# 512-column products in two steps of 256 columns

## Chip, cores and metric

The kernel runs on one core of one Trainium2 chip. The metric is the device time of one launch in microseconds (us), lower is better. Instruction times come from one profiled execution. A core has five engines that run side by side and wait for one another through semaphores: TensorE (PE, matrix products; its loads of the stationary operand are listed apart as PEld), VectorE (DVE), ScalarE (ACT), GpSimd (POOL) and SyncE (SP, which here issues the DMAs).

## The reference

One decoder layer on a sequence of 512 tokens of width 1024, in float32. Two groups of attention heads read the same normalised input through one projection; their outputs are concatenated and go through one output projection; a gated channel mixer of width 2816 follows.

```python
h = rms_norm(x, attn_pre_norm[l])
mix = hybrid_mixer(h, l, w_in[l], ..., w_out[l])   # proj = h @ w_in; two head groups; concat @ w_out
x = x + rms_norm(mix, attn_post_norm[l])
h = rms_norm(x, ffn_pre_norm[l])
f = (jax.nn.silu(h @ w_gate[l]) * (h @ w_up[l])) @ w_down[l]
x = x + rms_norm(f, ffn_post_norm[l])
```

## The kernel before

**Products in three terms.** Each float32 operand is split into a rounded part ("hi", type fp32r, made by ScalarE) and the rest ("lo", made by VectorE). A product of two operands is then three matmuls into the same accumulator: hi·hi, lo·hi and hi·lo. A matmul multiplies a stationary operand of 128 × 128 (loaded by a weight load of its own, so each matmul in the profile has one) with a moving operand of 128 partitions and up to 512 columns, and adds the result to a PSUM tile of 128 × 512, which is one bank. Eight such tiles exist (tag "b", `ps`).

**Order.** The kernel writes out its order by hand: `PLAN` and `PLAN_NORM` are lists of step names, and `run` calls one Python function for each, in that order, on all engines. Behind the colon of a step stand the slots that its tiles take, so every tile has a fixed address. Two steps that follow each other on one engine are executed in the order of the list; between engines, semaphores order reads and writes of tiles.

**Stages**, by the times of the profile:

- *Input projection* (6 to 126 us). The transposed input, 8 slices `xh[k]`/`xl[k]` of 128 × 512, is the moving operand; the weights are stationary. For the first six output tiles (`FIRST`) the weights come in blocks by slice k, and `product_piece` (L572) makes one matmul per step `F{m}.{c}.{k}`: tile m, term c, slice k. For the ten others, `product_fm` (L589) makes the 8 matmuls of one term per step `F{m}.{c}`. Among these run matmuls of the compressed keys (L804, 256 columns) and, in the other orientation with weights moving, the value projections (L705, 256 or 280 columns).
- *Attention* (to about 250 us): scores (L922, L923), transposes (L953), products with the values (L1136 and others). Four tiles of the output projection's first half are made here by `mix_part` (L1207, steps `M0` to `M3`): 12 matmuls of 512 columns each, from `MIX_A`, which `mix_keep` then copies out.
- *Output projection* (250 to 284 us): `mix_piece(i, k)` calls `mix_final` (L1221) for one row block i and one slice k; for each half c of the 1024 output columns it makes the three terms. Row blocks 0 and 1 take the four slices that `mix_part` left out, 2 and 3 all eight (`MIX_K`).
- *Gate and up projections* (284 to 500 us): `block` (L1474) in a scheme that needs seven instead of eight block products per pair. Its moving operands have 256 columns already.
- *Down projection* (from 493 us): `product` (L1548) makes two PSUM tiles (t = 0, 1) of three terms each from a pair of feature tiles, called by `product_a` four times and by `product_b` three times for each of nine pairs. The last four feature tiles go through `down` (L1697): one row block i, one half c, three terms. The pieces of the last quarter are made by `down_piece` (L1703), which has 256 columns already. Then sums, the norm and the output follow on VectorE and ScalarE (L1719 to L1755).

**Flags.** A matmul with `start=True` begins a bank anew: columns that are written first afterwards are set, not added to. So where two matmuls begin the two halves of a bank, only the first has the flag; L1474 does so already.

Of the kernel before, what the change touches and what calls it, by code (L numbers as in the profile page):

```python
# [17 lines left out]
P = 128  # L18
# [3 lines left out]
NK = D_MODEL // P  # L22
# [16 lines left out]
NF = D_FF // P  # L39
# [209 lines left out]
MIX_A = (0, 1, 4, 5)  # L249
# [4 lines left out]
NA = 2  # L254
WB = (3, 3, 3)
HALVES = ((0, 256), (256, 512))
LAST = 1
SLOT = 1.43
AHEAD = 3
# [25 lines left out]
def hybrid_block_kernel(  # L285
# [6 lines left out]
    act, dve, pool, pe = nc.scalar, nc.vector, nc.gpsimd, nc.tensor  # L292
# [101 lines left out]
    def sslot(name, dt=F32R):  # L394
        return S.tile([P, SEQ], dt, tag="s", name=name)
# [6 lines left out]
    def ps(name, dt=F32):  # L402
        return PS.tile([P, SEQ], dt, tag="b", name=name)
# [11 lines left out]
    raws, fms = {}, {}  # L415
    st = {}
# [125 lines left out]
    blk = {}  # L542
# [24 lines left out]
    def product_piece(m, c, k):  # L567
        first = ("fm", m) not in st
        if first:
            st["fm", m] = ps(f"fm{m}")  # L570
        w, xx = ((1, xh), (2, xh), (1, xl))[c]
        pe.matmul(st["fm", m], blk[k][w][:, m * P:(m + 1) * P], xx[k], start=first, stop=True, skip_group_check=True)  # L572

    def high_fm(m):
        hi = wpool.tile([P, 1024], F32R, tag="hi", name="whi", bufs=WB[1])
# [8 lines left out]
    def product_fm(m, c):  # L584
        if c == 0:
            st["fm", m] = ps(f"fm{m}")
        w, xx = ((0, xh), (1, xh), (0, xl))[c]
        for k in range(NK):
            pe.matmul(st["fm", m], fms[m][w][:, k * P:(k + 1) * P], xx[k], start=(c == 0 and k == 0),  # L589
                      stop=(c == 2 and k == NK - 1))  # L590

    wide_of = {}

# [52 lines left out]
    for pair in range(8):  # L646
        scale = SCALE if pair in (DQ0, DQ1, NQ0, NQ1) else 1.0
        for half in range(2):
            m = 2 * pair + half
# [330 lines left out]
    oth, otl = {}, {}  # L980
# [218 lines left out]
    wos = [None] * NK  # L1199
    mixp, mixq, mixw = [None] * (2 * NT), {}, [None] * 2  # L1200

    def mix_part(m, c):
        i, n = m // 2, 0
        pt = mixq[m] = ps("mixp")
        for k in MIX_A:
            for o, wi in ((oth, 0), (otl, 0), (oth, 1)):
                pe.matmul(pt, o[k][:, i * P:(i + 1) * P], wos[k][wi][c], start=(n == 0), stop=(n == 3 * len(MIX_A) - 1))  # L1207
                n += 1

    def mix_keep(m):  # L1210
        if mixw[m // 4] is None:
# [4 lines left out]
    def mix_final(i, mix, kts, first, last):  # L1216
        for c in range(2):
            n = 0
            for k in kts:
                for o, wi in ((oth, 0), (otl, 0), (oth, 1)):  # L1220
                    pe.matmul(mix[c], o[k][:, i * P:(i + 1) * P], wos[k][wi][c],  # L1221
                              start=(first and n == 0), stop=(last and n == 3 * len(kts) - 1))
                    n += 1

    kst, opair = [None] * GROUPS, {}
    for h in range(DIFF_HEADS):
        c = h // 2
# [61 lines left out]
    CS = [slice(c * SEQ, (c + 1) * SEQ) for c in range(2)]  # L1289
# [254 lines left out]

    def product(acc, a, b, first, last):
        for t in range(2):
            for n, (x, y) in enumerate(((0, 0), (1, 0), (0, 1))):
                pe.matmul(acc[t], a[x][:, t * P:(t + 1) * P], b[y],  # L1548
                          start=(first and n == 0), stop=(last and n == 2))

    accs, oa, ob, back4, ffx = {}, [{} for _ in range(NF)], [{} for _ in range(NPAIR)], {}, {}
    part, wc = {}, {}
# [137 lines left out]
    def quarter(i, c):  # L1690
        return accs[((1, 5), (7, 6))[i > 1][c]][i % 2]

    def down(f, i, c):
        o = HS * (i < 2) + (i % 2) * P
        first = f == 2 * NPAIR and c == 1 and i > 1
        for n, (a, wi) in enumerate(((0, 0), (1, 0), (0, 1))):
            pe.matmul(quarter(i, c), ffx[f][a][:, o:o + P], oa[f]["w"][wi][:, CS[c]],  # L1697
                      start=(first and n == 0), stop=(f == (NF - 3 if (i, c) == (LAST, 0) else NF - 1) and n == 2))

    def down_piece(f, h):  # L1700
        o = HS + LAST % 2 * P
        for n, (a, wi) in enumerate(((0, 0), (1, 0), (0, 1))):
# [11 lines left out]
    def piece(t, h):  # L1714
        return t if h is None else t[:, HALVES[h][0]:HALVES[h][1]]

# [6 lines left out]
    def out_tiles(i):  # L1723
        if i not in wc:
            wc[i] = [cpool.tile([P, 4], F32, tag="ssc", name="ss", bufs=NT), sslot("uf", F32), sslot("uf", F32)]
            if not junk and i in (0, LAST):
                junk.extend(sslot("uj", BF16) for _ in range(2))
        return wc[i]

    def last_square(i, c, h=None):  # L1730
        out_tiles(i)
        j = (1 - c) + (h or 0)
        sq = junk[c] if i in (0, LAST) else wc[i][1 + c].bitcast(BF16)
        act.activation(piece(sq[:, :SEQ], h), piece(part[i, c], h), AF.Square,
# [7 lines left out]
    def last_root(i):  # L1742
        r = cpool.tile([P, 1], F32, tag="rsc", name="rs", bufs=NT)
        j = 1 + (i == LAST)
        rsqrt_last(r, wc[i][0][:, j:j + 1], 1.0 / D_MODEL, wc[i][0][:, 3:4])
        wc[i].append(r)

    def last_gain(i, c):
        u = out_tiles(i)[1 + c]
        (nc.gpsimd if (i, c) == (LAST, 1) else dve).tensor_tensor(u, part[i, c], gains[2][:, CS[c]], OP.mult)  # L1750

# [64 lines left out]
    for f in range(NF + 1):  # L1816
        order = ((6, f), (5, f), (4, f - 1), (7, f), (3, f), (1, f + 1), (2, f + 1))
        for j, (n, ff) in enumerate(order):
            t = f * T + j * SLOT
            if (n, ff) == (4, NF - 1):  # L1820
                t = f * T - SLOT
# [3 lines left out]
    for f in range(NF):  # L1825
        b = f * T
# [23 lines left out]
    for p in range(NPAIR):  # L1850
        b = (2 * p + 2) * T
# [8 lines left out]
    for p in range(NPAIR):  # L1860
        b = te + 4 * p * D - 7.0
# [16 lines left out]
    for p in range(NPAIR):  # L1878
        b = tb + p * 3 * D - 6.0
# [19 lines left out]
    for f in range(2 * NPAIR, NF):  # L1899
# [3 lines left out]
        b = tc_ + (-15, -8, -3, 2)[g]  # L1903
# [3 lines left out]
    n = 0  # L1907
# [4 lines left out]
    for i in (2, 3, 0, 1):  # L1912
        for c in (1, 0):
# [8 lines left out]
            t = tc_ + n * D / 2  # L1922
# [3 lines left out]
            for h in pieces or (None,):  # L1926
                a = () if h is None else (h,)
# [100 lines left out]
```

## Time and profile before

| | us |
|---|---|
| median of three runs | 617.48 |
| lowest and highest | 616.74, 618.58 |
| profiled execution | 616.08 |
| its span, first to last instruction | 614.3 |

| engine | busy us | share of the span | instructions |
|---|---|---|---|
| PE | 604.1 | 98% | 4065 |
| PEld | 547.6 | 89% | 4065 |
| DVE | 545.9 | 89% | 965 |
| ACT | 373.4 | 61% | 784 |
| POOL | 101.5 | 17% | 153 |

The profile page shows these and the chain of work that ended last: at each step it goes back to what released an instruction, or to the instruction ahead of it on its engine. 86% of that chain is PE, 8% DVE, 3% DMA. Matmuls are pipelined: one starts before the one ahead of it has ended, so the sum of durations is more than the time they take, and the distance between starts is what counts. The mean granted clock of TensorE is 0.998.

### The profile page before, as it was taken

What the parts mean: (1) busy time and instruction counts of PE and PEld (TensorE: products, weight loads), DVE (VectorE), ACT (ScalarE), POOL (GpSimd) and SP (SyncE); (2) the same over time, 40 slices, a digit from 0 to 9 for tenths busy, and PEclk for the clock granted to TensorE, in tenths of its full rate; (3) what the DMA queues carried; (4) which work ended last, traced back from release to release, by engine and by line L of the source; (5) the groups of instructions that cost most, each with busy time, mean ns of one, the idle gap of its engine ahead of it and who ended that gap; (6) DMA issues with size and microseconds to landing.
All of it is one profiled execution on the core that took longest, in us unless ns stands there. A gap on an engine that the chain in (4) does not pass through costs nothing.

```text
span 614.3 us, 11002 instructions
## 1 busy us (share of the span) xinstructions
PE 604.1 (98%) x4065; PEld 547.6 (89%) x4065; DVE 545.9 (89%) x965; ACT 373.4 (61%) x784; POOL 101.5 (17%) x153
## 2 busy tenths in 40 slices
PE   8999999999999999999999999999999999999995
PEld 5888888899999989889999999999999978888884
DVE  5888988997899885899999999899999899989977
ACT  6436365476898986568585645555554566667522
POOL 0030000306868789200000000000000000000000
PEclk9999999999999999999999999999999999999999
DMA  8557788656342311644253443335342554576413
GB/s 260 194 196 276 272 271 283 230 189 208 105 120 87 103 36 35 206 171 147 94 159 117 138 138 123 119 125 184 122 138 86 172 172 161 185 247 230 137 41 132
DMA packets 38341, 98.41 MB, mean 160 GB/s; under 512 B 4240, under 2 KB 11792, under 8 KB 37392
## 3 DMA queue, kind: packets, MB, share of 16 engines
q1 hardware_dynamic: 38144, 97.59, 47.6%
q8 instruction: 32, 0.52, 0.3%
q14 instruction: 21, 0.17, 0.1%
q10 hardware_dynamic: 144, 0.13, 0.1%
HBM read 82.10 MB, written 15.60 MB: 159 GB/s over the span
## 4 chain that ended last, share of the span: by engine, by line
PE 86%; DVE 8%; DMA 3%; ACT 1%; issue 1%; SPq 0%; DVEq 0%
PE yz L1474 25%; PE acc L1548 13%; PE fm L589 9%; PE mix L1221 5%; PE x L1474 4%; PE fm L572 4%; PE tr L953 4%; PE avn L1136 3%; PE g L705 2%; PE sc L922 2%; PE sc L923 2%; PE mixp L1207 2%; PE v L705 2%; PE cmp L804 1%; PE av L1014 1%; PE acc L1697 1%
## 5 line engine op out<-in xcount | busy, mean ns | idle before, releaser
L1750 POOL TENSOR_TENSOR uf<-c,gain 128x512 f32<-128x512 f32 x1 | 1.3, 1283 | 353.4 <-DVE c L1719 353.4
L936 ACT ACTIVATE p<-sc,nm 128x256 f32<-128x256 f32 (+3 forms) x96 | 50.2, 530 | 13.8 <-DVE nm L932 13.5
L1474 PE MATMUL yz<-rope,wbh 128*128 128x256 f32 x352 | 47.1, 276 | 0.0
L932 DVE TENSOR_REDUCE nm<-sc 128x1 f32<-128x384 f32 (+3 forms) x96 | 42.9, 481 | 4.3 <-PE sc L928 3.7
L1105 POOL TENSOR_TENSOR p<-p,l 128x256 f32<-128x256 f32 (+3 forms) x64 | 45.3, 732 | 0.9
L1474 PEld LDWEIGHTS yz<-rope,wbh 128*128 128x128 f32 x352 | 43.2, 188 | 0.0
L966 DVE TENSOR_TENSOR ptl<-tr,pth 128x384 fp32r<-128x384 f32 (+1 forms) x60 | 34.2, 590 | 8.9 <-ACT pth L963 8.7
L963 ACT ACTIVATE pth<-tr 128x384 fp32r<-128x384 f32 (+1 forms) x60 | 30.3, 528 | 6.8 <-PE tr L953 6.5
L1451 ACT ACTIVATE wbh<-wraw 128x1024 fp32r<-128x1024 f32 x22 | 23.3, 1057 | 11.8 <-DVE wraw L1438 7.5
L1451 ACT ACTIVATE weh<-e 128x1024 fp32r<-128x1024 f32 x22 | 23.2, 1056 | 11.7 <-DVE e L1433 7.3
L1451 ACT ACTIVATE whi<-wraw 128x1024 fp32r<-128x1024 f32 x22 | 23.1, 1054 | 11.2 <-DMA wraw<-in_wg 9.9
L1459 DVE TENSOR_TENSOR wel<-e,weh 128x1024 fp32r<-128x1024 f32 x22 | 26.7, 1217 | 2.5 <-ACT weh L1451 2.4
L953 PE MATMUL tr<-ident,p 128*128 128x128 f32 x200 | 27.7, 273 | 0.0
L1597 ACT ACTIVATE whi<-wraw 128x1024 fp32r<-128x1024 f32 x20 | 21.0, 1056 | 11.0 <-PE acc L1548 4.1
L1459 DVE TENSOR_TENSOR wbl<-wraw,wbh 128x1024 fp32r<-128x1024 f32 x22 | 26.8, 1217 | 0.7 <-ACT wbh L1451 0.5
L1474 PE MATMUL yz<-rope,wbl 128*128 128x256 f32 x176 | 27.1, 276 | 0.0
L1459 DVE TENSOR_TENSOR wlo<-wraw,whi 128x1024 fp32r<-128x1024 f32 x22 | 26.8, 1218 | 0.2 <-ACT whi L1451 0.2
L1603 DVE TENSOR_TENSOR wlo<-wraw,whi 128x1024 fp32r<-128x1024 f32 x20 | 24.1, 1220 | 2.5 <-ACT whi L1597 2.5
L1474 PEld LDWEIGHTS yz<-rope,wbl 128*128 128x128 f32 x176 | 23.2, 188 | 0.0
L1504 ACT ACTIVATE us<-yz 128x512 f32<-128x512 f32 x22 | 13.0, 589 | 16.9 <-PE yz L1474 16.5
L953 PEld LDWEIGHTS tr<-ident,p 128*128 128x128 f32 x200 | 22.4, 141 | 0.8
L922 PE MATMUL sc<-kst,qst 128*128 128x384 f32 (+3 forms) x64 | 22.8, 365 | 0.0
(382 smaller groups left out, 1993.5 us busy)
## 6 DMA issues: line engine op xcount, KB each, us to landing
wraw<-in_wg SPq DMA_DIRECT2D x24, 512.0 KB, 3.6
wraw<-in_wu SPq DMA_DIRECT2D x22, 512.0 KB, 3.3
wraw<-in_wd SPq DMA_DIRECT2D x22, 512.0 KB, 3.8
qk<-rope SPq DMA_DIRECT2D x7, 1024.0 KB, 5.5
kst<-qk SPq DMA_DIRECT2D x24, 256.0 KB, 4.2
wraw<-in_wf SPq DMA_DIRECT2D x10, 512.0 KB, 4.4
wraw<-in_wo SPq DMA_DIRECT2D x8, 512.0 KB, 4.0
qst<-qk SPq DMA_DIRECT2D x16, 256.0 KB, 2.8
```

Of the source, the lines that this page charges most:

```text
L589: pe.matmul(st["fm", m], fms[m][w][:, k * P:(k + 1) * P], xx[k], start=(c == 0 and k == 0), stop=(c == 2 and k == NK - 1))
L922: pe.matmul(sv[i], lhs, kk[:, 0, :w], start=(n == 0), stop=False, skip_group_check=True)
L932: dve.tensor_reduce(nm[i], sv[i], AX.X, OP.max, negate=True)
L936: act.activation(pp[i], sv[i], AF.Exp, bias=nm[i], accum_out=hs["l"][:, row, i:i + 1])
L953: pe.transpose(tr[:, n * P:(n + 1) * P], pp[i][:, j * P:(j + 1) * P], ident)
L966: dve.tensor_tensor(part(u, 1), tv[u], f32(part(u, 0)), OP.subtract)
L1105: pool.tensor_tensor(p, p, hs["l"][:, 1 + br, i:i + 1].to_broadcast(list(p.shape)), OP.mult)
L1221: pe.matmul(mix[c], o[k][:, i * P:(i + 1) * P], wos[k][wi][c], start=(first and n == 0), stop=(last and n == 3 * len(kts) - 1))
L1451: act.activation(t[0], w[src], AF.Copy)
L1459: dve.tensor_tensor(t[1], W[f][PARTS[n][0]], f32(t[0]), OP.subtract)
L1474: pe.matmul(o, W[f][w][wi][:, k * P:(k + 1) * P], hop[h][hi][:, k * HS:(k + 1) * HS], start=(n < 3 and m == 0), stop=(m == 11), skip_group ...
L1548: pe.matmul(acc[t], a[x][:, t * P:(t + 1) * P], b[y], start=(first and n == 0), stop=(last and n == 2))
```

## The change

Six places that made one matmul of 512 columns now make two of 256, on the two halves of the same PSUM tile and of the same moving operand. The stationary operand is the same, and is loaded for each. In `product_piece` the two halves follow each other. In the other five the halves are an outer loop: first all terms (and slices) of the step for columns 0 to 255, then all for 256 to 511; `mix_part` and `mix_final` likewise around their loop over slices. Order of the steps, slots, buffers, DMAs and the work of the other engines are as before. The start flag goes to the first half alone.

```diff
+SIDES = tuple(slice(*h) for h in HALVES)
...
     def product_piece(m, c, k):
...
-        pe.matmul(st["fm", m], blk[k][w][:, m * P:(m + 1) * P], xx[k], start=first, stop=True, skip_group_check=True)
+        for s in SIDES:
+            pe.matmul(st["fm", m][:, s], blk[k][w][:, m * P:(m + 1) * P], xx[k][:, s],
+                      start=first and not s.start, stop=True, skip_group_check=True)
...
     def product_fm(m, c):
...
-        for k in range(NK):
-            pe.matmul(st["fm", m], fms[m][w][:, k * P:(k + 1) * P], xx[k], start=(c == 0 and k == 0),
-                      stop=(c == 2 and k == NK - 1))
+        for s in SIDES:
+            for k in range(NK):
+                pe.matmul(st["fm", m][:, s], fms[m][w][:, k * P:(k + 1) * P], xx[k][:, s],
+                          start=(c == 0 and k == 0 and not s.start), stop=(c == 2 and k == NK - 1), skip_group_check=True)
...
     def mix_part(m, c):
...
-        for k in MIX_A:
-            for o, wi in ((oth, 0), (otl, 0), (oth, 1)):
-                pe.matmul(pt, o[k][:, i * P:(i + 1) * P], wos[k][wi][c], start=(n == 0), stop=(n == 3 * len(MIX_A) - 1))
-                n += 1
+        for s in SIDES:
+            for j, k in enumerate(MIX_A):
+                for o, wi in ((oth, 0), (otl, 0), (oth, 1)):
+                    pe.matmul(pt[:, s], o[k][:, i * P:(i + 1) * P], wos[k][wi][c][:, s], start=(n == 0),
+                              stop=(j == len(MIX_A) - 1 and wi == 1), skip_group_check=True)
+                    n += 1
...
     def mix_final(i, mix, kts, first, last):
         for c in range(2):
             n = 0
...
+            for s in SIDES:
+                for j, k in enumerate(kts):
+                    for o, wi in ((oth, 0), (otl, 0), (oth, 1)):
+                        pe.matmul(mix[c][:, s], o[k][:, i * P:(i + 1) * P], wos[k][wi][c][:, s],
+                                  start=(first and n == 0), stop=(last and j == len(kts) - 1 and wi == 1),
+                                  skip_group_check=True)
+                        n += 1
...
     def product(acc, a, b, first, last):
         for t in range(2):
-            for n, (x, y) in enumerate(((0, 0), (1, 0), (0, 1))):
-                pe.matmul(acc[t], a[x][:, t * P:(t + 1) * P], b[y],
-                          start=(first and n == 0), stop=(last and n == 2))
+            for s in SIDES:
+                for n, (x, y) in enumerate(((0, 0), (1, 0), (0, 1))):
+                    pe.matmul(acc[t][:, s], a[x][:, t * P:(t + 1) * P], b[y][:, s],
+                              start=(first and n == 0 and not s.start), stop=(last and n == 2), skip_group_check=True)
...
     def down(f, i, c):
...
-        for n, (a, wi) in enumerate(((0, 0), (1, 0), (0, 1))):
-            pe.matmul(quarter(i, c), ffx[f][a][:, o:o + P], oa[f]["w"][wi][:, CS[c]],
-                      start=(first and n == 0), stop=(f == (NF - 3 if (i, c) == (LAST, 0) else NF - 1) and n == 2))
+        for s in SIDES:
+            for n, (a, wi) in enumerate(((0, 0), (1, 0), (0, 1))):
+                pe.matmul(quarter(i, c)[:, s], ffx[f][a][:, o:o + P], oa[f]["w"][wi][:, CS[c]][:, s],
+                          start=(first and n == 0 and not s.start),
+                          stop=(f == (NF - 3 if (i, c) == (LAST, 0) else NF - 1) and n == 2), skip_group_check=True)
```

More of the change, by code (lines that the diff above doesn't have):

```diff
@@ L1218, in mix_final @@
             n = 0
[L1219 to L1223, printed above, removed]
+            for s in SIDES:
[5 more added lines that the diff above has]
+                        n += 1
     kst, opair = [None] * GROUPS, {}
```

## The prediction

> **What bounds the kernel now.** First the table of stages, which gives for each stretch of the span the busy time of TensorE (PE), of its weight loads (PEld), of VectorE (DVE), ScalarE (ACT) and GpSimd (POOL), with the number of instructions, the granted clock, the DMA share and the rate.
>
> ```profile
> core 0: us, PE busy (x) PEld busy (x) DVE busy (x) ACT busy (x) POOL busy (x), PEclk, DMA share, GB/s
> ...
> 55.00:126.00 71.00, 71.00 (x374) 60.22 (x374) 61.78 (x107) 38.85 (x86) 5.37 (x7) 1.00 0.74 251
> ...
> 250.00:284.00 34.00, 34.00 (x158) 27.80 (x157) 31.81 (x59) 21.33 (x44) 2.16 (x2) 1.00 0.53 186
> 284.00:470.00 186.00, 185.98 (x1637) 185.54 (x1636) 178.51 (x264) 106.86 (x173) 0.00 (x0) 1.00 0.39 129
> ...
> 500.00:589.00 89.00, 89.00 (x387) 72.33 (x386) 81.36 (x122) 53.23 (x86) 0.00 (x0) 1.00 0.54 183
> 589.00:614.30 25.30, 18.16 (x85) 14.77 (x83) 19.73 (x46) 7.83 (x26) 1.28 (x1) 0.95 0.22 84
> ```
>
> TensorE is busy without a gap from 55 to 589 us, at the full clock. A busy TensorE need not be one at its peak, so I looked at who makes it wait. This is the list of its waits, whole: source, total in us, times, longest.
>
> ```profile
> PE warm L424 <- DVE warm L421: 1.2, 1, 1.2
> PE fm L572 <- ACT whi L562: 0.8, 1, 0.8
> PE acc L1548 <- DVE act L1493: 0.6, 1, 0.6
> PE cmp L804 <- DVE wlo L795: 0.3, 1, 0.3
> ```
>
> That is 2.9 us in 614.3. So between the waits the time is set by how fast matmuls follow one another, and the quantity that the change acts on is the distance from one matmul's start to the next. The chain that ended last, in order of time (start, duration, what, how many merged), shows that distance, because a merged piece divided by its count is one matmul's share:
>
> ```profile
> 6.49 19.73 PE fm L572 x85
> ...
> 55.33 11.20 PE fm L589 x48
> ...
> 69.00 9.17 PE fm L589 x40
> ...
> 80.86 7.47 PE fm L589 x32
> ...
> 90.43 9.18 PE fm L589 x40
> ...
> 215.87 2.79 PE mixp L1207 x12
> ...
> 249.50 22.25 PE mix L1221 x96
> ...
> 297.75 29.95 PE yz L1474 x264
> ...
> 499.42 79.99 PE acc L1548 x345
> ...
> 582.86 5.56 PE acc L1697 x24
> 588.44 0.70 DVE c L1719
> ```
>
> All lines but L1474 are the products that the change halves: 512 columns, at 232.1 ns (19.73/85) in L572, 231.4 in the four pieces of L589 (37.02/160), 232.5 in L1207, 231.8 in L1221, 231.9 in L1548, 231.7 in L1697. L1474 is not touched, and has 256 columns already: 29.95/264 = 113.4 ns. **Twice that is 226.9 ns, some 4 ns less than one product of 512 takes.** On this alone the change would pay. But the pieces of L589 already differ among themselves: 233.3, 229.3, 233.4 and 229.5 ns.
>
> **Two paces.** The timeline (start, time from the first start to the last end, engine, line, tiles, shape, count) shows this inside L589. From each row's start to the next row's start there are as many matmuls as the row counts.
>
> ```profile
> 57.03 2.03 PE L589 MATMUL fm<-xl,whi 128*128 128x512 f32 x8
> 58.90 2.26 PE L589 MATMUL fm<-xh,whi 128*128 128x512 f32 x9
> ```
>
> ```profile
> 72.51 2.00 PE L589 MATMUL fm<-xh,whi 128*128 128x512 f32 x8
> 74.34 1.99 PE L589 MATMUL fm<-xh,wlo 128*128 128x512 f32 x8
> ```
>
> (58.90−57.03)/8 = 234 ns in the first, (74.34−72.51)/8 = 229 ns in the second: same line, same shape, no wait. The 256-column matmuls of the other lines that stay as they are have two paces as well. In the answers for one source line (engine, op, tiles, count: shortest/median/longest duration in ns, first and last start, shapes):
>
> ```profile
> L705 PE MATMUL v<-whi,xl x32: 281/281/281, 40.9 to 51.2; 128*128 128x256 f32 x32
> ```
>
> ```profile
> L705 PE MATMUL v<-whi,xl x32: 276/276/281, 142.5 to 183.4; 128*128 128x256 f32 x32
> ```
>
> ```profile
> L804 PE MATMUL cmp<-whi,chl x32: 274/281/287, 53.6 to 101.1; 128*128 128x256 f32 x32
> ```
>
> ```profile
> L1703 PE MATMUL acc<-whi,ffl x4: 276/276/276, 605.8 to 606.8; 128*128 128x256 f32 x4
> ```
>
> ```profile
> L1474 PE MATMUL yz<-rope,wbh x352: 276/276/302, 305.7 to 492.9; 128*128 128x256 f32 x176
> ```
>
> A duration of 276 goes with the 113.4 ns of L1474. What 281 goes with, the timeline of L705 says:
>
> ```profile
> 41.86 0.63 PE L705 MATMUL v<-whi,xh 128*128 128x256 f32 x4
> ...
> 45.16 0.64 PE L705 MATMUL v<-whi,xl 128*128 128x256 f32 x4
> ```
>
> Seven rows of four lie from the one to the other: 3.30 us/28 = 117.9 ns. So a 256-column matmul goes at about **113.4 or 117.8 ns**, a 512-column one at about **229 or 233.4 ns**, and a pace is kept over many matmuls. No view says what chooses: L705 has the same line and shape at both, and so has L589.
>
> **The change, part by part.** Steps that become two: L572 144 (6 tiles × 3 terms × 8 slices), L589 240 (10 × 24), L1207 48 (4 × 12), L1221 144 (two row blocks with 4 slices, two with 8, × 2 halves × 3 terms), L1548 378 (9 pairs × 7 products × 6), L1697 90 (30 pieces × 3): 1044 products. Added are 1044 matmuls and 1044 weight loads; no DMA, no buffer, no work on another engine.
>
> Their time now: 144 × 232.1 + 240 × 231.4 + 48 × 232.5 + 144 × 231.8 + 378 × 231.9 + 90 × 231.7 = 242.1 us. A piece of the chain includes what happens at its edges, so I take 231 ns inside the streams, about midway between the two paces: 241.2 us.
>
> Afterwards, all at 113.4: 1044 × 226.8 = 236.8 us, **−4.4 us**. All at 117.8: 1044 × 235.6 = 246.0 us, **+4.8 us**. Those are the ends. Break-even is at 115.5, a little over half at the slow pace. The difference of 4.4 ns comes once per matmul in both sizes (233.4−229 and 117.8−113.4): after the change it can come twice per product.
>
> Which share? Where the trace has 256 columns in the stages that change, 96 of L705 are slow, the other 96 are mostly quick, L804's 64 are mostly slow, L1703's 12 are quick: some 45% quick. L1474 is nearly always quick, with 1848 of them. I take 55%, nearer to the rows beside the changed lines, since the changed products read the same tiles as these: 0.55 × 113.4 + 0.45 × 117.8 = 115.4 ns, 230.8 per product, 240.9 us: **−0.3 us**.
>
> The extra weight loads cost nothing more, because each is hidden under the matmul ahead of it; the page shows them for the untouched line:
>
> ```profile
> L1474 PEld LDWEIGHTS yz<-rope,wbh 128*128 128x128 f32 x352 | 43.2, 188 | 0.0
> ```
>
> One load per matmul is in the 113.4 ns. The Trainium skill, "TensorE: Matmul & The Clock Gate", section "LDWEIGHTS (loading the stationary operand)", gives columns/1.2, so 107 ns a load, and Part 3 of the page lets a load overlap a running matmul only where the row group differs; by that reading 1044 loads would add 111 us. The stage of L1474 does not agree: a load of 107 and 256 columns cannot follow one another in 113.4 ns. The same 284–470 us show that two instructions per 113 ns can be issued for 186 us without a stall.
>
> Other edges: the third term's "lo" tile is needed after two half steps instead of two whole ones, some 0.23 us sooner. The list of waits has only one wait at a changed product that is new on the chain (L1548, 0.6 us, for L1493), so I cost that at nothing; without that cover it is 0.23 us each time. The last half step ends a tile as the whole one did. DVE would not take over in 500–589: with all 387 quick the stage shrinks by some 1.7 us to 87.3, above DVE's 81.4. From 588.44 on the chain is DVE's, so what the last products gain or lose (some 70 × 4 ns = 0.3 us) may not reach the end.
>
> **The rivals.** *The quick pace nearly everywhere.* For: L1474 keeps it over 1848 matmuls with all kinds of tiles, L1703 is the halved form of L1697 itself, and the changed streams are long. Against: L705's first 96. At 85% quick: 114.1 ns, 238.2 us, −3.0 us.
>
> *The slow pace nearly everywhere: slower.* The second 4.4 ns per product is then paid almost always. It decides from 69% slow (116.4 ns, 243.1 us). For: L705 and L804 at 40–101 us, which read tiles of the same kinds, and that L1207, L1221 and L1697 stand nearer 233.4 than 229 now. Against: L1474, L1703. At 85% slow: 117.1 ns, 244.6 us, +3.4 us.
>
> *Each step carries a fixed cost of its own: slower too.* Two slow halves take 235.6 ns where a slow whole takes 233.4; if that 2.2 ns were the price of any further step, the change would cost 1044 × 2.2 = 2.3 us. Against: two quick halves take 226.8, less than the quick whole's 229. The Trainium skill, "TensorE: Matmul & The Clock Gate", section "Wait — 56ns, not 53.3ns?", has such a rule: 2.5 ns per matmul on top of its columns at the full clock; an estimate by it is 1044 × 2.5 = 2.6 us more. The slow rows fit it, the quick rows do not.
>
> *It does not reach the end.* In 250–284 DVE is busy 31.81 of 34.00 us; a gain of 144 × 4 ns = 0.6 us would leave 33.4, so only little cover is left, and in 589–614 the chain is DVE's. A gain could be lost there, and the time would stay at 617.5.
>
> **How the numbers follow.** The profiled execution took 616.08 us (span 614.3 and 1.8 around it); the median of the three runs is 617.48, and I forecast against the median. About 0.3% (1.85 us) is what a measurement of this kernel can tell from no change. It is reached at 70% quick (114.7 ns, 229.4, 239.5 us) on the one side and at 31% on the other.
>
> - Forecast, mixed paces (31 to 70% quick): 617.48 − 0.3 = 617.2; its own range 615.6 to 619.3; chance 0.52
> - Quick nearly everywhere: 617.48 − 3.0 = 614.5; chance 0.27
> - Slow nearly everywhere: 617.48 + 3.4 = 620.9; chance 0.12
> - A fixed cost per step: 617.48 + 2.3 = 619.8; chance 0.05
> - Does not reach the end: 617.5; chance 0.04
>
> Faster 0.27, same 0.52 + 0.04 = 0.56, slower 0.12 + 0.05 = 0.17. The range leaves a tenth out on each side: 614.3 to 620.2.
>
> **What would show it.** Right: in the changed profile the halves of all six lines have durations near 276 and 281 mixed, pieces of the chain divide to 115–116 ns, and TensorE's waits stay near 3 us. Nearly all at 276 and 113.4 means the first rival, nearly all at 281 and 117.8 the second. Wrong altogether: a third pace, weight loads that end waits of TensorE, or new waits at the first product of a group.

## The result: slower by 1.1%

The changed kernel takes **623.57 us** (median of 6 runs, 622.27 to 625.28), the kernel before beside it 616.89 us: a ratio of 1.0114, 95% interval 1.0098 to 1.0129. That is 6.7 us more by the two medians and 7.0 by the ratio; costs in us below go by the ratio. The forecast of 617.2 us was wrong, and its range ended at 620.2. The profiled execution took 622.92 us with a span of 621.1, 6.8 more than the span of before; the granted clock is as before (0.998).

First the durations. In the answers for one source line of the changed kernel (duration shortest/median/longest in ns), two halved lines and one line that was left alone:

```profile
L574 PE MATMUL fm<-xl,whi x96: 277/279/282, 5.9 to 41.2; 128*128 128x256 f32 x96
...
L1707 PE MATMUL acc<-whi,ffl x28: 281/281/281, 592.2 to 611.0; 128*128 128x256 f32 x28
...
L709 PE MATMUL v<-whi,xl x64: 276/276/281, 41.8 to 185.8; 128*128 128x256 f32 x64
```

The halves sit at 279 to 281, the untouched L709 (L705 before) at 276. Its matmuls up to 51 us were at 281 before, so a line that the change leaves alone changed its pace too. What that means for the distance of starts is in the chain that ended last of the changed kernel (start, duration, what, how many merged):

```profile
71.06 9.42 PE fm L593 x80
...
83.17 7.54 PE fm L593 x64
...
92.58 9.07 PE fm L593 x80
...
228.97 2.83 PE mixp L1212 x24
...
252.66 22.61 PE mix L1228 x192
...
301.48 30.19 PE yz L1482 x264
...
395.33 5.51 DMA wraw<-in_wg
408.48 5.14 DMA wraw<-in_wu
...
504.94 2.46 PE acc L1557 x19
507.42 78.51 PE acc L1557 x671
...
589.46 10.60 PE acc L1707 x90
```

Divide: 117.8 ns in two pieces of L593 and **113.4 in a third**, 117.9 in L1212, 117.8 in L1228, 117.0 in L1557, 117.8 in L1707. So most halves go at the slow pace and a few at the quick one; no piece shows a third pace. All six long pieces of L593, 368 matmuls, take 43.04 us on this chain, 117.0 each. With 117.8 for L574, twice these paces against the figures of the chain of before (232.1, 231.4, 232.5, 231.8, 231.9, 231.7) gives 144 × 3.5 + 240 × 2.5 + 48 × 3.3 + 144 × 3.8 + 378 × 2.1 + 90 × 3.9 = 3.0 us; against the 231 that the prediction took inside the streams, 3.8 us. **By this reckoning about half of the 6.8 us is the pace.**

Part of the rest is in the waits. The list of TensorE's waits, of the changed kernel (source, total in us, times, longest):

```profile
PE warm L425 <- DVE warm L422: 1.2, 1, 1.2
PE cmp L808 <- DVE wlo L799: 0.7, 1, 0.7
PE acc L1557 <- DVE act L1501: 0.7, 1, 0.7
PE cmp L808 <- DVE chl L787: 0.6, 1, 0.6
PE yz L1482 <- DVE wel L1467: 0.6, 1, 0.6
PE fm L574 <- ACT xh L445: 0.6, 1, 0.6
PE yz L1482 <- DVE vs L1517: 0.4, 1, 0.4
PE mixp L1212 <- POOL ol L1163: 0.3, 1, 0.3
```

Eight entries and 5.1 us, four and 2.9 us before: 2.2 us more, so 0.8 to 1.6 us stand in neither account. Two of the new ones stand at L1482 (L1474 before), a line that the change does not touch. The same stage shows it in its place: L1474's longest piece began at 297.75 and the long piece of L1548 at 499.42; now these starts are 301.48 and 504.94. The stage between, with no halved product, grew by 1.8 us (a second profile of the kernel before has 0.8 us of that as well). Ahead of its stalls the chain above has loads of 5.51 and 5.14 us, where the chain of before had TensorE.

One more row changed that the prediction did not look at. The table of DMA queues of the page, before and after (packets, MB, share):

```profile
q8 instruction: 32, 0.52, 0.3%
```

```profile
q8 instruction: 40, 0.66, 0.4%
```

0.52 MB in 32 packets are 16 KB each, and the page counts them, like the weights, as a share of the 16 DMA engines. 2088 instructions more on TensorE make eight packets more; 768 more on GpSimd (e16, below) add none to this row. So these packets are TensorE's stream of instructions.

Every experiment below has one profile. To compare them, a ledger was worked out from the traces: VectorE's instructions are the same in all kernels, and the start of each was set against its start in the kernel before; the median shift near four places gives what each stretch lost (us):

```
                                       to 130  130-296  296-504  504-600   all
the program before, a second time        0.4     -0.1      0.8      0.0     1.1
changed kernel                           2.2      1.5      1.8      1.2     6.7
changed kernel, a second time            0.1      1.5      2.6      1.1     5.3
e1   halves in the projections          -0.3      0.2      1.2      0.0     1.2
e18  the same again                      2.0      0.2      2.2      0.0     4.3
e3   halves in L1548                    -1.2     -0.1      1.9      0.9     1.5
e8   halves in L1207, L1221, L1697       0.5      1.3      2.3      0.2     4.3
e7   change, operands moved              4.0      1.9      1.7      1.9     9.6
e10  change, halves adjacent             1.5      0.8      1.1      0.7     4.1
e2   e1, operands moved                 -0.2      0.5      1.3     -0.3     1.3
e6   operands moved alone               -0.2      0.6      0.4     -0.3     0.6
e9   idle instructions everywhere        1.3      0.0      0.6      0.0     1.8
e15  idle in the projections             1.2     -0.1      1.9      0.0     3.0
e19  the same again                      1.2      0.0      2.4      0.0     3.6
e17  idle in L1548                      -1.3     -0.1      1.7     -0.1     0.2
e16  idle on GpSimd                     -1.4     -0.1      0.5      0.0    -1.0
e12  128 idle                            0.6     -0.1     -0.3      0.0     0.2
e13  256 idle                            0.0      0.0      0.6      0.0     0.6
e14  change, 128 idle                    1.6      1.4      2.2      1.2     6.4
```

Between executions of one kernel the second and the fourth stretch repeat to 0.1 us; the third differs by 0.5 to 1.0 us, and the first scatters by a microsecond or two, so single entries there prove little. The verdicts below go by the medians of the timed runs, and use the ledger to say where.

### The profile page after: what moved, and what is told of

The parts are those of the page before. It is cut to its first block, busy times and chain, and to the rows that moved or that the text cites. A ratio compares the mean times of both kernels' runs of the same rounds, so it can differ in the third digit from the quotient of the medians.

```text
span 621.1 us, 13095 instructions
## 1 busy us (share of the span) xinstructions
PE 608.9 (98%) x5109; PEld 597.0 (96%) x5109; DVE 546.5 (88%) x965; ACT 373.9 (60%) x784; POOL 101.7 (16%) x153
## 4 chain that ended last, share of the span: by engine, by line
PE 75%; DVE 11%; DMA 8%; POOL 2%; issue 2%; ACT 1%; SPq 0%; DVEq 0%; ACTq 0%; POOLq 0%
PE yz L1482 18%; PE acc L1557 14%; PE fm L593 7%; PE mix L1228 5%; PE fm L574 3%; PE x L1482 3%; PE tr L957 3%; PE avn L1140 3%; PE acc L1707 3%; DMA wraw<-in_wu 2%; PE g L709 2%; PE v L709 2%; PE sc L926 2%; PE sc L927 2%; PE mixp L1212 2%; DMA wraw<-in_wf 2%
## 5 line engine op out<-in xcount | busy, mean ns | idle before, releaser
L1482 PE MATMUL yz<-rope,wbh 128*128 128x256 f32 x352 | 47.2, 276 | 0.0
L1482 PEld LDWEIGHTS yz<-rope,wbh 128*128 128x128 f32 x352 | 43.2, 188 | 0.1
L1482 PE MATMUL yz<-rope,wbl 128*128 128x256 f32 x176 | 27.1, 276 | 0.0
L1482 PEld LDWEIGHTS yz<-rope,wbl 128*128 128x128 f32 x176 | 23.2, 188 | 0.0
```

The lines of the kernel that those rows point to most:

```text
L1482: pe.matmul(o, W[f][w][wi][:, k * P:(k + 1) * P], hop[h][hi][:, k * HS:(k + 1) * HS], start=(n < 3 and m == 0), stop=(m == 11), skip_group ...
```

## Experiments: the parts

Two theories stood against each other. *Pace*: all of the loss is the second 4.4 ns of each product. *Stream*: some of it is due to the 2088 instructions as such, wherever the halves are quick or slow.

**The projections alone** (e1), and the products of L1548 alone (e3):

```diff
 # e1: product_piece and product_fm as in the change, all else as before
+        for s in SIDES:
+            pe.matmul(st["fm", m][:, s], ..., xx[k][:, s], ...)
```

```diff
 # e3: product as in the change, all else as before
+            for s in SIDES:
+                for n, (x, y) in enumerate(((0, 0), (1, 0), (0, 1))):
+                    pe.matmul(acc[t][:, s], ..., b[y][:, s], ...)
```

> Only the input projection's 384 products (L572, L589 of the kernel before) are halved. Pace theory (a half goes at 117.8 ns mostly, as in the changed kernel: 117.8 in its first part, 116.9 in its second): 288 x 117.8 + 480 x 116.9 = 90.0 us against 88.4 before, so 1.6 to 2.5 us slower with the stalls at its edges. Fixed cost per step (2.2 ns): 0.8 us slower. Instruction-fetch theory (the stalls come from 133 KB more of TensorE instructions): 384 of 1044 steps, so about a third of the changed kernel's extra stalls, and the slow weight loads at 44 to 60 us are there again.

> Only the 378 products of L1548 are halved. Pace theory: 756 x 116.7 against 378 x 230.8, so 1.0 us slower. Fixed cost: 0.8 us slower. Instruction-fetch theory: no more stalls before 490 us, as nothing is added there; in the SwiGLU stage no wait for the weights beyond those of before.

e1: 617.76 us, ratio 1.0030 (1.0019 to 1.0041), 1.8 us more. e3: 617.84 us, 1.0029 (1.0019 to 1.0040), 1.8 us more. For e3 the chain gives 80.88/690 = 117.2 ns:

```profile
500.03 80.88 PE acc L1550 x690
```

But the ledger puts only 0.9 us of e3's loss behind 504 us, and 1.9 between 296 and 504, where nothing that runs was changed. Some of that is scatter: the kernel before, profiled a second time, loses 0.8 us there, and e3 gains 1.2 ahead of 130 us, also without a change. Still, that stretch became the clue.

**The other three lines alone** (e8; a first form, e5, gave no measurement), 282 products:

```diff
 # e8: mix_part, mix_final and down as in the change, all else as before
```

> The kernel before with the halves in the output projection (mix_part, mix_final) and the down projection (down) alone: 282 products. If the distance between starts is all of the price, these three lines gain what they gained in the whole change, 0.68 + 0.63 + 0.37 = 1.7 us, the ratio is 1.002 to 1.003, and the three parts (this one, the projections alone, the products of the SwiGLU stage alone) add up to some 5.2 us, 1.5 us less than the whole change's 6.7. If each part carries new waits in proportion to its instructions, this one is 2.0 to 2.5 us slower and the three parts add up to the whole.

620.39 us, ratio 1.0056 (1.0038 to 1.0074): 3.5 us for the smallest of the three parts, where the reckoning above gives these lines 1.1 us of pace (1.3 against 231 ns). With 1.8 and 1.8 the parts add up to 7.1 us, the whole change's 7.0 (a second measurement of e1, below, gives more); but the loss does not go by the number of products.

**The address.** A gap of 128 bytes ahead of the pool of activations was left out, so every tile in that pool starts 128 bytes lower, the projection's moving operands among them; tiles of the weights' pool stay: with e1 (e2), alone (e6), with the whole change (e7).

```diff
-    nc.gpsimd.memset(G2.tile([P, 32], F32, name="gap2"), 0.0)
```

> As e1, and the 128 bytes of padding (and its one GpSimd memset) ahead of the pool that holds the projection's moving operands are left out, so that these begin at 128 modulo 256 bytes, with the stationary ones at 192, which is how the SwiGLU stage's operands lie. Address theory (where the moving operand lies decides the pace): the halves go at 113.4 ns, the projection takes 768 x 113.4 = 87.1 us in place of 90.0, so about 3 us faster than e1 and 0 to 1.5 us faster than before. If the pace is chance or phase alone: as e1, 1.6 to 2.5 us slower than before.

> No product halved; only the gap of 128 bytes ahead of the activations' pool is left out, so every moving operand in it starts 128 bytes lower. If the operand's address chooses between the two distances, whole products go nearer to 229 than to 233 ns in L1548 (some 87.9 us in place of 88.3, as in the run with halved projections and the gap left out), and the time is 0.5 to 1.5 us below the kernel before. If the address does nothing, the lines' totals are those of the kernel before within 0.2 us and the ratio is 1.000.

> The whole change, with the gap of 128 bytes left out as well. If the halves lose because they sit at 117.8 ns, and the address of the moving operand decides on that, the projections (L572, L589) come down by some 1.3 us and the products of L1548 go below 115.5 ns each; the time is 2 to 4 us below the whole change's 623.6. If the loss is a fixed cost of a step or of its instructions, the time stays at 623 to 624 whatever the address.

The pace does follow the address. The same 64 halves in the chain of e1, and of e2:

```profile
80.68 7.54 PE fm L593 x64
```

```profile
81.15 7.27 PE fm L592 x64
```

117.8 ns became 113.6. Counted from the start times in the traces, without the stalls, 13% of the projections' halves are quick (a distance of at most 115.5 ns) in the changed kernel and in e1 (3% in e18, which is e1 again), 59% in e2 and 73% in e7. But L1548's halves, a mixture in the changed kernel, went slow in e7:

```profile
107.02 5.46 PE fm L592 x48
...
507.06 81.72 PE acc L1556 x690
```

113.8 and 118.4 ns. It is not the moving operand's address alone: among the slowed are products whose moving tile lies in the weights' pool and stayed (`whi` with `s4r`, 115.5 ns in the changed kernel, 117.8 in e7); there only the stationary tile moved. Nor is it addresses alone: a piece of 80 matmuls of L593 that took 9.07 us in e1 (113.4 each) took 9.42 (117.8) in e18. No time was won: e2 617.85 us (e1 617.76), e6 617.30 us, ratio 1.0012 (1.0002 to 1.0021), e7 624.54 us, 1.0128 (1.0109 to 1.0147). So addresses have a part in choosing the pace, one move does not make all lines quick, and what e7 gained in pace in the projections did not lower its time: its ledger has 4.0 us ahead of 130 us. Pace alone does not explain the loss.

**The order inside a product** (e10): the halves of one product directly behind each other, so that each tile is needed where it was needed before.

```diff
-            for s in SIDES:
-                for n, (x, y) in enumerate(((0, 0), (1, 0), (0, 1))):
+            for n, (x, y) in enumerate(((0, 0), (1, 0), (0, 1))):
+                for s in SIDES:
                     pe.matmul(acc[t][:, s], ...)
 # and likewise in product_fm, mix_part, mix_final and down
```

> The whole change with the halves of one product directly behind each other, so that each tile is needed at the same place in the order as before; steps, instructions and addresses are those of the change. If the earlier need of the third term's tile makes the new waits, they go and the time falls by 1 to 3 us below the whole change's 623.6. If the steps' distance and their number make the loss, the time stays at 622.5 to 624.5.

621.78 us, ratio 1.0082 (1.0058 to 1.0106), between the two cases. The whole change, run beside it, took 622.76 us, 1.0118 (1.0088 to 1.0148); the intervals overlap. The place is clearer: between 130 and 296 us the change loses 1.4 to 1.5 us in three profiles and e10 0.8, and the wait of L1212 for GpSimd's `ol` (0.3 us in both profiles of the change, and in e8) is gone from the list. With the halves as the outer loop, the first tile of the output projection needs its last `ol` tile before GpSimd has made it: some 0.6 us. The timelines show the first and the eleventh matmul of that tile, before and after:

```profile
215.63 0.48 PE L1207 MATMUL mixp<-wh,oh 128*128 128x512 f32 x1
...
218.03 0.39 PE L1207 MATMUL mixp<-whi,ol 128*128 128x512 f32 x1
```

```profile
218.08 0.36 PE L1212 MATMUL mixp<-wh,oh 128*128 128x256 f32 x1
...
219.79 0.38 PE L1212 MATMUL mixp<-whi,ol 128*128 128x256 f32 x1 [0.30 <-POOL ol L1163]
```

The tile was needed 2.40 us behind the first matmul; ten half steps make it some 1.2.

> The whole change once more, for a second profile of it. If the new gaps belong to the change, the gaps between matmuls are again some 12 us (8.7 and 10.0 in two profiles of the kernel before), with waits at the compression and in the SwiGLU stage; if they belong to one execution, they come near 10 us and the time of this profiled execution is 1.5 to 2 us less than 622.9.

The change's second profile has TensorE waiting at L1482 again, 1.1 us for `wel` and 0.4 for `vs`, and none at the compression:

```profile
PE yz L1482 <- DVE wel L1467: 1.1, 1, 1.1
PE acc L1557 <- DVE act L1501: 0.7, 1, 0.7
PE yz L1482 <- DVE vs L1517: 0.4, 1, 0.4
```

So the waits at the compression are not in every execution of the change. That for `vs` is no mark of the change either: the kernel before, profiled a second time (e4), has 0.5 us of it at the same line. Only the wait for `wel` stands in both profiles of the change and in neither of the kernel before.

## Experiments: the stream without the halves

**Idle instructions on TensorE** (e9): whole products, and two instructions behind each that do nothing, 2088 in all. A first attempt (e4) used a form that was gone from the program that ran (11002 instructions and 32 packets, as before); it only gave the kernel before once more, 615.88 us.

> The kernel before, whole products, with two no-ops on TensorE's queue behind each of the 1044 products: as many instructions as the changed kernel has, in the same places, and no matmul more. Pace theory: within 0.5 us of before. Instruction-fetch theory: 1.5 to 2.5 us slower, with weight loads of 5 us at 44 to 60 us and in the SwiGLU stage and matmuls of 512 columns at 229 to 233 ns as before.

```diff
                 pe.matmul(acc[t], a[x][:, t * P:(t + 1) * P], b[y], ...)
+                for _ in range(2):
+                    pe.nop(hint="x")
 # and behind the products of the five other lines
```

> The kernel before, whole products of 512, with two instructions that do nothing behind each of them on TensorE: as many instructions more as the change adds (2088), and no step halved. If the longer stream of instructions is what the stalls come from (more instruction packets among the loads, 40 in place of 32, loads that land later, new waits), its packets go to 40, the gaps between matmuls grow by some 3 us and the time is 2 to 4 us above the kernel before. If the stream costs nothing, the packets go to 40 and the time stays within 0.5 us.

```profile
q8 instruction: 40, 0.66, 0.4%
```

The packets go to 40, and the time to 619.32 us, ratio 1.0047 (1.0031 to 1.0064): **2.9 us with no product halved** (the profiled execution of e9 took 617.92 us, below its median; its ledger shows 1.8 us, 1.3 of it ahead of 130 us, and where the rest falls no profile shows). The paces are those of before: whole products of L1548 and L1697 start 230.7 ns apart on average, stalls left out, 230.8 in the kernel before. So a part of the loss has nothing to do with the distance of halves.

**Where in the stream.** Is it the place at which packets come? 128 idle instructions early on move all later packets by half a packet (e12), 256 by a whole one (e13), 128 in the changed kernel bring them back in the SwiGLU stage (e14).

```diff
+    idle = [False] * 80 + [True] * 64      # e13: 16 and 128
...
         pe.matmul(st["fm", m], blk[k][w][:, m * P:(m + 1) * P], xx[k], ...)
+        if idle.pop():
+            pe.nop(hint="x")
+            pe.nop(hint="x")
```

> The kernel before with 128 idle instructions in TensorE's stream: two behind each of the first 64 products of L572. An instruction packet holds 256 instructions, so from there on the packets come half a packet away from where they came in the program before; their number grows by a half. If it is the place of the packets among the loads that costs, this takes 1 to 3 us more than before, like the 2088 idle instructions (2.9 us), though it has a sixteenth of them. If it is their number that costs, it takes 0.0 to 0.3 us more.

> The kernel before with 256 idle instructions: two behind each of the first 128 products of L572, a whole packet. From there on the packets come at the places in the program where they came before. If the place costs, this takes less than 0.7 us more than before; if the number costs, 0.2 to 0.5 us; if any idle instruction in the first stage costs, twice what the 128 cost.

> The whole change with 128 idle instructions in the same way (two behind each of the first 64 products). Up to the SwiGLU stage the change adds 1152 instructions, four packets and a half; with 128 more it is five, so in the stage of L1474 and at the start of L1548 the packets come where they came before the change. If the place costs, the time falls by 1 to 2 us below the change's 623; if the number costs, it stays or rises by 0.2 us.

e12 617.40 us, ratio 1.0013 (0.9999 to 1.0028); e13 616.72 us, 1.0001 (0.9985 to 1.0016); e14 622.11 us, 1.0097 (1.0069 to 1.0126), not distinguishable from the change. So a shift of half a packet does not cost what the 2088 instructions cost: e12 loses at most 1.7 us by its interval. That the place does nothing is not shown, and one load in the projections, below, shows that it does something.

**Idle instructions in one part**: the projections (e15), L1548 (e17), and GpSimd in its idle 353 us (e16).

```diff
 # e15: two pe.nop(hint="x") behind each product of product_piece and product_fm
 # e17: two behind each product of product
 # e16, once, at the first call of product:
+        while idle:                        # 768 entries
+            pool.nop(hint=idle.pop())
```

> The kernel before with two idle instructions behind each product of the projections alone (384 products, 768 instructions, three whole packets). If the place of packets costs, only the projections lose by it (their packets come at other places) and later stages do not: 0.3 to 1.5 us more. If the number costs in proportion, 768/2088 of 2.9 us: 1.1 us more, and the later stages are as before too. Beside the halves in the projections alone (1.7 us more) it tells how much of those is the stream's and how much the steps' distance (0.95 + 0.70 - 0.42 us by the trace).

> The kernel before with two idle instructions behind each product of the SwiGLU stage alone (378 products, 756 instructions); up to 497 us every engine runs what it ran before. If the length of the program makes the loads later wherever they are, the 38 loads of the stage ahead of these products take 3.7 us on average, and the time rises by 1 to 3 us, some of it ahead of 497 us. If packets cost where they come, those loads stay at 3.6 us and whatever is lost is lost behind 497 us.

> The kernel before with 768 idle instructions in GpSimd's stream, where that engine has no work (between its step of the output projection and its one step near the end, 353 us idle); TensorE's stream is that of before, and its packets stay at 32. If a program that is longer in memory is what makes the loads land later (38 weight loads of the SwiGLU stage: 3.50 to 3.62 us on average in the programs of 32 and 33 packets, 3.71 to 3.92 in all longer ones), they go to 3.7 us and the time rises by 1 to 3 us. If only TensorE's own stream does it, they stay at 3.6 us and the time within 0.7 us.

e15 619.25 us, ratio 1.0050 (1.0032 to 1.0067), 3.1 us: as much as e9 with nearly three times the instructions. e17 616.32 us, 1.0010 (1.0000 to 1.0021). e16 615.74 us, 0.9995 (0.9986 to 1.0004): GpSimd's longer stream, six packets more in another row of the queues (27 for 21), costs nothing here. Two places come out of this.

*The projections.* Up to 126 us five packets come in the kernel before and eight in e15, in the same time. Rows of the DMA view for 6 to 126 us, and for the load of `in_wf` that is issued near 43 us (KB, us from issue to landing), first before, then e15:

```profile
q8 instruction: 5, 0.08, 0.3%
...
wraw<-in_wf SPq DMA_DIRECT2D x1, 512.0 KB, 3.6
```

```profile
q8 instruction: 8, 0.13, 0.5%
...
wraw<-in_wf SPq DMA_DIRECT2D x1, 512.0 KB, 5.3
```

What this load holds up is in the chain of the changed kernel, between 44 and 56 us: the tiles made of it stand in VectorE's queue ahead of `chl` and `wlo`, which the compression (L808) needs.

```profile
44.06 5.28 DMA wraw<-in_wf
...
49.36 1.07 ACT whi L579
...
50.46 1.23 DVE wlo L584
...
54.00 0.68 DVE chl L787 x2
54.68 1.14 DVE wlo L799
```

And e15's list of waits has them:

```profile
PE cmp L810 <- DVE chl L789: 1.2, 1, 1.2
PE cmp L810 <- DVE wlo L801: 0.7, 1, 0.7
```

Over all profiles: where the projections have 768 instructions more or a few over, this load took 4.4 to 5.3 us in eight of eleven (3.4 and 3.5 in the others, e1, e14 and the change's second); in the nine other profiles 3.2 to 3.6. The packets' start times in the traces tell the cases apart without overlap. In the eight a packet started 1.0 to 2.3 us behind the issue of this load; in the twelve others 2.8 us behind it or later, or none came while it ran. The same kernel stands on both sides: in the changed kernel's first profile a packet came 1.1 us into the load, which took 5.3 us, in its second 2.8 us into it and it took 3.5. So here the place of the packets counts, and more packets in the same time make such a meeting likelier. What it costs in time is less clear: by the ledger e2 lost nothing ahead of 130 us with a load of 4.6 us, and e14 lost 1.6 with one of 3.5.

*The SwiGLU stage.* e17 runs up to 497 us what the kernel before runs, and its profile still loses 1.7 us between 296 and 504. By the timed runs it costs 0 to 1.3 us in all: the same profile gains 1.3 us ahead of 130, where the scatter is. The loads of that stage are longer. Rows of the DMA view for 295 to 470 us (count, KB, median us to landing): before, e16, e17:

```profile
q8 instruction: 12, 0.20, 0.5%
...
wraw<-in_wu SPq DMA_DIRECT2D x19, 512.0 KB, 3.3
```

```profile
wraw<-in_wu SPq DMA_DIRECT2D x19, 512.0 KB, 3.2
```

```profile
q8 instruction: 12, 0.20, 0.5%
...
wraw<-in_wu SPq DMA_DIRECT2D x19, 512.0 KB, 3.5
```

The mean over the stage's 38 weight loads, from issue and landing in the trace, separates the kernels without overlap: 3.50 to 3.62 us in the six with at most 256 instructions more on TensorE, 3.71 to 3.92 us in the fourteen with 564 and more. In the ledger the first group loses 0.8 us at most in that stretch, the second 0.6 to 2.6, so in time the two groups just overlap. The stage is fed just in time: VectorE is busy 178.51 of its 186 us, and TensorE waits for what it makes of these loads. Meetings with packets are not the whole of it: over the loads in which no packet started 0.5 to 2.5 us behind the issue, the means are 3.45 to 3.59 us in the first group and 3.62 to 3.83 in the second. Why loads land later when TensorE's stream is longer *behind* the stage is not settled.

**The halves in the projections and the idle instructions there, side by side.** e1 had cost 1.8 us and e15 3.1, on two chips, though e1 has the slow halves as well.

> The halves in the projections alone, once more, now on one chip with the idle instructions in the projections. They cost 1.8 us the first time, and the idle instructions, as many and in the same places, 3.1 us, though these change no distance between matmuls. If the difference came of the two chips, both cost the same here, within 1 us, or the halves more by the steps' distance (1.2 us). If idle instructions cost something that real ones do not, the halves come to 1.8 us again and the idle ones to 3.1.

> Two idle instructions behind each product of the projections, once more, on one chip with the halves there: 3.1 us again if it is the kernel, 0.5 to 1.5 us if the first measurement was its chip's. In the profile the load of in_wf that is issued near 43 us lands in 4.6 to 5.3 us where the time is lost, and in 3.2 to 3.6 us where it is not.

On one chip: halves 619.54 us, ratio 1.0050 (1.0033 to 1.0067), idle instructions 619.17 us, 1.0047 (1.0031 to 1.0063); 3.1 and 2.9 us, and the load near 43 us took 4.8 and 4.4 us. So e1's first figure was not repeated, and whether the chip or the scatter of the first stretch made it is not settled; in e18's profile a packet came 1.0 us into that load, in e1's 2.8. Run together the two are alike within the intervals: these runs do not separate a pace of 1 us in the projections from none.

## Why the prediction was wrong

**The bound was read rightly as far as it went**: TensorE's distance between starts. The two paces of 256 columns, the price of each and the break-even at 115.5 ns stand, though at 115.5 ns a little under half of the halves are slow (48%), not a little over. (The sum of the products' times before is 242.0 us, not 242.1; nothing rests on it.) For whole products 229 and 233.4 are means of pieces: single distances in the trace lie between 225 and 237 ns. By the prediction's own signs the durations of 279 to 281 spoke for its second rival, and waits of 5.1 us went against "stay near 3 us".

**First step that failed: "I take 55%"** for the quick share. By the paces above the 1044 pairs take 234.6 ns in the mean, 117.3 a half, which is the price of some 10% quick; by single start distances 381 of the 2088 halves, 18%, are quick. That is the second rival, *the slow pace nearly everywhere*: it was priced at 3.4 us for 85% slow, and the reckoning gives 3.0 to 3.8. No rows of the kernel before told this share. By start distances the 256-column rows that the prediction named in the changed stages were about a third quick (91 of 267; it read some 45%), L1474 97%, and the very products that were to be halved about half at 231 ns or less (560 of 1044). Addresses move the share (e2, e7), and so does the execution (e1, e18); what sets it is open. In the stretches that repeat, the price can be read off in time: 0.7 to 0.8 us of the output projection's 1.4, and 0.7 to 1.2 us behind 504. In the projections, the remaining 1.1 to 1.4 us of the reckoning, it was not shown in time.

**Second: "Added are 1044 matmuls and 1044 weight loads; no DMA, no buffer, no work on another engine."** There was a DMA: eight instruction packets more. The loads of the stationary operand are hidden, as the prediction said (the untouched L1482 still shows 30.19/264 = 114.4 ns, small stalls included), so it was right that they cost TensorE nothing. But the instructions as such cost 2.9 us (e9, 1.9 to 3.9). In e9's profile the load of `in_wf` near 43 us took 4.7 us, and TensorE waited 1.0 us at the compression (0.3 before). Later loads become waits where there is little slack: the prediction's own table has VectorE busy 178.51 of 186 us in the untouched stage. No rival had this mechanism. The Trainium skill, "Runtime: NRT & Kernel Launch", section "Instruction fetch mechanics", says that a sequencer fetches its stream through a DMA queue of its own in blocks of 16 KiB, and that crossing a block is mostly hidden. The 16 KB are what the rows give. TensorE's own pace agrees with hidden (230.7 and 230.8 ns above, and e17 loses nothing behind 504 us with three packets more); what is not hidden here is that loads beside them land later.

**Third: "some 0.23 us sooner", and then the edges at nothing.** Two half steps for two whole ones hold for L1548 and L1697, with three matmuls a step. In `mix_part` the halves stand around all twelve, so the last `ol` is needed some 1.2 us sooner. That cost some 0.6 us in the output projection; behind 504 us the change and e10 differ by 0.5 us (1.2 and 0.7), but there e10's pace is a little quicker too (80.48/690 = 116.6 ns on its chain).

Pace 3.0 to 3.8, edge 0.6 and stream 2.9 make 6.5 to 7.3 us, against 7.0 measured. The sum fits, but loosely: with e9's interval it is 5.5 to 8.3. The terms are not independent measurements of the change either: the stream's is that of idle instructions, and e18 and e19 show that in the projections stream and pace do not simply add.

**The other rivals.** The fixed cost per step (2.2 ns, 2.3 us) is too small for the whole, and the third piece of L593, at 113.4 ns a half, goes against it. "Quick everywhere" did not happen in any run. No version here beats the kernel before: its nearest are e16 and e13, which are it but for instructions that do nothing.

## What to carry to other kernels

When a change splits one operation into two, count the instructions as traffic: here each 256 more on TensorE are a packet of 16 KB among the loads, and where a stage is fed just in time a few tenths of a microsecond on each load can become waits. Idle instructions on the engine in question measure that price without the change. When a trace shows two paces for one shape and no view says what chooses, do not take the share from neighbours: neither rows of the same shape nor the undivided products of the same operands gave it here. Price both ends, and give the slow end its weight. And when halves become an outer loop, count for each tile how many steps sooner it is needed, over the whole loop.

## What was not expected of the hardware

- Two paces of one shape, turned by addresses: 64 halves at 117.8 ns went at 113.6 when their moving operand started 128 bytes lower (e1, e2), while another line of the same kernel went from 117.0 to 118.4 (e7). Addresses are not all: the same kernel ran 80 halves at 113.4 ns in one profile and at 117.8 in another (e1, e18).
- A load of 512 KB that takes 4.4 to 5.3 us when a packet of TensorE's instructions starts 1.0 to 2.3 us behind its issue, and 3.2 to 3.6 when one starts later or none comes (20 profiles).
- Loads that land later under a longer stream of TensorE, even one that is longer only behind them: a median of 3.5 us for the same 19 loads of 512 KB that have 3.3 in the kernel before (e17), and 3.2 with 768 idle instructions on GpSimd (e16). The cause stays open.
